# Projections cut into steps among local attention and level products in the second mixer of a two-block transformer kernel

## The chip, the cores and the metric

The kernel runs on one core of a Trainium2 chip, as one program. Time is device time in microseconds (us) of one execution. The profile is of one execution, taken by the hardware profiler; its times are microseconds from the start of the span unless a number is marked ns.

## What is computed

The input x has 512 positions of width 1024. A first block has a mixer (forgetting attention and chunked attention), attention over 256 memory rows and a feed-forward part. A second block has a mixer (below) and a layer that picks 16 x 8 of 16384 experts for each position. The change concerns the start of the program, where the memory rows are normed and projected, and the mixer of the second block:

```python
proj = h @ w_in[l]
aq, ak, av, gq, gk, gv, gg, glr = jnp.split(proj, split_points, axis=-1)
att = sliding_window_attention(aq, ak, av, attn_sinks[l])      # 8 heads, window 128
log_a = jax.nn.log_sigmoid(glr @ gla_gate_up[l] + gla_gate_bias[l]) / GLA_TAU
go = gla_chunked(gq, gk, gv, log_a)                            # 4 heads, linear attention with decay
go = rms_norm(go, gla_norm_w[l]).reshape(B, S, GLA_V_W) * jax.nn.silu(gg)
mixed = jnp.concatenate([att, go], axis=-1) @ w_out[l]
```

In `gla_chunked` position t takes from position s <= t the value of s by q_t . k_s times a decay, in each key channel the exponential of the difference of the summed log gates b at t and at s.

## The kernel before

Everything is in float32. A projection is three matmuls of float32r parts, high by high, low by high and high by low (`mm3`, lines 70 to 74), so each weight chunk that lands in `wraw` is first split: ScalarE copies the high part (`whi`, line 65), VectorE subtracts (`wlo`, line 66). `proj_T` gives transposed results: a chunk of 256 output columns is two groups of 8 x 3 matmuls with 512 moving columns, each into one PSUM bank, followed by a ScalarE copy (`evac`). `proj_rows` gives rows: for each of four 128-row tiles 8 x 3 matmuls. PSUM's eight banks are named by use: three `mm`, two `lg`, two `pt`, one `pv`. A bank is waited for when its turn comes again.

The code is written in program order; a scheduler that works when the kernel is built turns it into one fixed list of instructions for each engine, and an engine takes its list in order. What the lists are is shown below for three places.

**The second mixer** (`mixer2`). In the order of the code: two chunks of projections (key, gate input, `gq`), one for `gk`, the summed log gates `b`, two chunks of values (lines 751 to 754), the first query chunk (chunk 3), then for each half h: for h = 1 the second query chunk (chunk 4), and eight steps of `window` (local attention; two head pairs by four query tiles), each followed by one step of the generator `gla`, then two more steps of `gla`. Last come the two gate chunks 5 and 6 (`gg`), each followed by `silu_times`, and the split of the eight result tiles for the output projection (`row_hl`, lines 124 to 128).

A step of `window` (lines 659 to 699) does two logit matmuls, on VectorE a masked reduction, minimum, sum, reciprocal and scale, on ScalarE the exponentials, then transposes, a copy and the value matmuls. Eight steps of `gla` (lines 558 to 584) make the decay-weighted scores of 128 by 128 tiles: the diagonal first, and then seven levels. At level m = 1, 2, ... 64 a tile falls into blocks of 2m; pairs with t in the upper and s in the lower half of a block are this level's. The code takes the difference of b to the middle of the block for all positions (GpSimd, line 566), its absolute value and the exponential of minus that (ScalarE, 567 and 568), multiplies q by it (VectorE, 570) and k by it (GpSimd, 572), forms all 128 by 128 products for four tiles and two heads (TensorE, 578), and copies those of the level by a mask (VectorE, 583). The last two steps form the states that pass from tile to tile, the outputs and their norm (lines 587 to 634).

**The start.** `mem_kv` (line 388) sends the gain row g_mem_kv, then each memory tile, on SP's queue; the scheduler puts two weight chunks of w_mk ahead of the tiles. Each tile is squared (ScalarE, 93), normed (VectorE, 104), transposed (TensorE, 119), and split (ScalarE 121, VectorE 122) before w_mk is multiplied.

Of the kernel before, what the change touches and what calls it, by code (L numbers as in the profile page):

```python
# [8 lines left out]
F32 = mybir.dt.float32  # L9
# [9 lines left out]
S = 512  # L19
# [20 lines left out]
class Net:  # L40
# [89 lines left out]
    def proj_T(self, ws, x, nt, evacs, tags=("mm", "mm")):  # L130
# [127 lines left out]
    def mixer(self, hT):  # L258
        nc, a = self.nc, self.a
        with ExitStack() as c:  # L260
# [17 lines left out]
            def val(name, i):  # L278
# [5 lines left out]
                        [evac("fq", ch) for ch in range(2)], ("mm", "lg"))  # L284
# [103 lines left out]
    def mem_kv(self, mk_d, mv_d, between):  # L388

        nc, a = self.nc, self.a  # L390
        g = self.bcast_row(self.gain, a["g_mem_kv"], D, "gain", nc.sync)
        with ExitStack() as c:
            mp = c.enter_context(self.tc.tile_pool(reuse_waits="tile", name="memT", bufs=1))
            mT = Cols(mp, 2, tag="mT")
            for t in range(2):
                m = self.row.tile([128, D], F32, name="rowt")
                nc.sync.dma_start(m, a["mem"][0, t * 128:(t + 1) * 128, :])
                self.to_T(self.norm(m, g, None, m), mT, t)
# [5 lines left out]
            for ch in range(4):  # L404
                self.proj_T([self.weights(a["w_mk"][ch])], mT, 2, [evac(ch)])
# [8 lines left out]
    def mem_attention(self, hT, mk, mv):  # L414
        nc, a = self.nc, self.a
        with ExitStack() as c:
# [7 lines left out]
            self.proj_T([self.weights(a["w_mq"][ch]) for ch in range(2)], hT, NT, [evac(0), evac(1)], ("mm", "lg"))  # L424
# [30 lines left out]
    def feed_forward(self, hT, g, side, then):  # L455
        nc, a = self.nc, self.a
        with ExitStack() as c:
# [5 lines left out]
            for gr in range(8):  # L463
# [10 lines left out]
                if gr == 0:  # L474
                    self.proj_T(ws, hT, NT, [evac(0), evac(1)], ("mm", "lg"))
# [75 lines left out]
    def gla(self, qT, kT, b, v, gnw, outs, big, pp):  # L551
# [3 lines left out]
        for i in range(2):  # L555
            att = pp.tile([128, 2, NT, 128], F32, name="att", bufs=1)
            bi = b[:, i, :]
            for lev in range(-1, 7):
                if lev < 0:
                    ql, kl = qT[i], kT[i]  # L560
                else:
                    m = 1 << lev
                    e = pp.tile([128, S], F32, name="ge")
                    bv = bi.rearrange("p (n w) -> p n w", w=2 * m)
                    ev = e.rearrange("p (n w) -> p n w", w=2 * m)
# [3 lines left out]
                    ql = pp.tile([128, S], F32, name="gql")  # L569
                    nc.vector.tensor_mul(ql, qT[i], e)  # L570
                    kl = pp.tile([128, S], F32, name="gkl")
                    nc.gpsimd.tensor_mul(kl, kT[i], e)
                pss = [self.bank("mm").rearrange("p (a b) -> p a b", a=NT) for _ in range(2)]
# [5 lines left out]
                for j, ps in enumerate(pss):  # L579
                    if lev < 0:  # L580
                        nc.vector.tensor_mul(att[:, j], ps, self.ident[:, None, :].to_broadcast([128, NT, 128]))
                    else:
                        nc.vector.copy_predicated(
                            att[:, j], self.levmask[:, lev:lev + 1, :].to_broadcast([128, NT, 128]), ps)
                yield

            qb = pp.tile([128, S], F32, name="gql")
# [5 lines left out]
            kd = pp.tile([128, S], F32, name="gkl")  # L593
# [5 lines left out]
            kdT = pp.tile([128, NT - 1, 128], F32, name="ge")  # L599
# [16 lines left out]
            for j in range(2):  # L616
# [11 lines left out]
                sq = pp.tile([128, S], F32, name="gkl")  # L628
# [7 lines left out]
    def silu_times(self, o, g, pp):  # L636

        nc = self.nc
        e = pp.tile([128, S], F32, name="ge")
# [704 lines left out]
```

## Time and profile before

| | |
|---|---|
| median of three runs | 2433.2 us (2431.38 to 2435.75) |
| the profiled execution | 2440.6 us |
| its span | 2438.1 us |
| busy in the span: TensorE, VectorE, ScalarE, GpSimd | 97%, 72%, 41%, 23% |
| mean granted TensorE clock | 0.985 of full speed |

The profiled execution is 2.5 us longer than its span, for what lies around it. Busy time is a union of instruction times; matmuls overlap and their ends are modelled, so that the spacing of starts tells more than the length of one. The granted clock has two levels, 1.2 and 2.4 GHz; a share between 0.5 and 1 in a stretch is a mix of them.

### The profile page before, as it was taken

The page shows a single profiled execution, that of the slowest core. Times are in us where ns is not written, and L with a number is a line of the kernel's source. Part 1 is how long each engine was busy: PE and PEld are TensorE (multiplying, and loading weights), DVE is VectorE, ACT ScalarE, POOL GpSimd, SP SyncE. Part 2 cuts the span into 40 slices and gives each one's busy share as a digit, 9 for nine tenths or more (in the row PEclk, how much of TensorE's full clock was granted, in tenths as well). Part 3 has the DMA queues.
Part 4 walks back from the last instruction along what each step waited for, and adds up shares of the span by engine and source line. Part 5 has one row for each costly group of instructions (what it writes and reads, how often), then busy time and mean ns, then how long its engine had stood idle before and what let it go on. Part 6 is the DMA issues. An engine that isn't in the chain of part 4 may idle for free. (4 is left out here: it accounts for less than half of the span.)

```text
span 2438.1 us, 33761 instructions
## 1 busy us (share of the span) xinstructions
PE 2355.7 (97%) x12339; PEld 2005.8 (82%) x12339; DVE 1750.0 (72%) x3670; ACT 1010.1 (41%) x1656; POOL 550.8 (23%) x518
## 2 busy tenths in 40 slices
PE   6999999999999998998999899999999999999998
PEld 6866668788788887677988899888888888888887
DVE  5344554476565465766899999998988887988874
ACT  5344543443433334553333666433333343333332
POOL 2021010010010011212220000343434444444420
PEclk9999999999999999879999999999999999999999
DMA  6422223145454222013333455999888999999972
GB/s 259 139 87 70 70 104 108 48 182 201 178 193 152 97 76 87 18 35 143 101 113 125 184 215 213 335 322 328 298 308 325 348 342 346 340 351 335 334 286 77
DMA packets 163909, 479.83 MB, mean 197 GB/s; under 512 B 14968, under 2 KB 72328, under 8 KB 147488
## 3 DMA queue, kind: packets, MB, share of 16 engines
q1 hardware_dynamic: 119520, 317.76, 36.7%
q0 software_dynamic: 44224, 159.93, 18.2%
q8 instruction: 97, 1.59, 0.3%
q14 instruction: 68, 0.56, 0.1%
HBM read 438.85 MB, written 38.77 MB: 196 GB/s over the span
## 5 line engine op out<-in xcount | busy, mean ns | idle before, releaser
L65 ACT ACTIVATE whi<-wraw 128x1024 fp32r<-128x1024 f32 x430 | 446.9, 1048 | 650.5 <-PE hidT L73 288.2
L66 DVE TENSOR_TENSOR wlo<-wraw,whi 128x1024 fp32r<-128x1024 f32 x414 | 501.9, 1220 | 239.6 <-ACT whi L65 223.8
L72 PE MATMUL hidT<-hThi,whi 128*128 128x384 f32 x1024 | 346.5, 338 | 1.0 <-ACT aside L1030 1.0
L73 PE MATMUL hidT<-hTlo,whi 128*128 128x384 f32 x1024 | 345.1, 337 | 0.0
L74 PE MATMUL hidT<-hThi,wlo 128*128 128x384 f32 x1024 | 344.4, 336 | 0.0
L74 PE MATMUL o<-whi,al 128*128 128x512 f32 x768 | 300.6, 392 | 0.0
L73 PE MATMUL o<-wlo,ah 128*128 128x512 f32 x768 | 300.3, 391 | 0.0
L72 PE MATMUL o<-whi,ah 128*128 128x512 f32 x768 | 298.9, 389 | 1.1 <-ACT ah L1082 1.1
L967 POOL DMA_INDIRECT rows<-peer_u,ei x128 | 170.2, 1330 | 492.9 <-DVE ei L960 262.2
L967 POOL DMA_INDIRECT rows<-peer_v,ei x128 | 173.3, 1354 | 205.3 <-DVE ysparse L988 179.5
L73 PE MATMUL mm<-hTlo,whi 128*128 128x512 f32 (+1 forms) x560 | 207.8, 372 | 4.2 <-DVE hTlo L122 4.2
L72 PE MATMUL mm<-hThi,whi 128*128 128x512 f32 (+1 forms) x560 | 208.3, 374 | 1.7 <-ACT hThi L121 1.5
L74 PE MATMUL mm<-hThi,wlo 128*128 128x512 f32 (+1 forms) x560 | 208.1, 372 | 0.0
L72 PEld LDWEIGHTS hidT<-hThi,whi 128*128 128x128 f32 x1024 | 192.5, 188 | 4.8 <-ACT aside L1030 1.4
L73 PEld LDWEIGHTS hidT<-hTlo,whi 128*128 128x128 f32 x1024 | 192.4, 188 | 3.3
L74 PEld LDWEIGHTS hidT<-hThi,wlo 128*128 128x128 f32 x1024 | 192.3, 188 | 0.1
L74 PEld LDWEIGHTS o<-whi,al 128*128 128x128 f32 x768 | 144.0, 188 | 30.7 <-DVE al L1084 0.6
L72 PEld LDWEIGHTS o<-whi,ah 128*128 128x128 f32 x768 | 144.2, 188 | 29.8 <-ACT ah L1082 1.8
L73 PEld LDWEIGHTS o<-wlo,ah 128*128 128x128 f32 x768 | 144.1, 188 | 28.3
L988 DVE SCALAR_TENSOR_TENSOR ysparse<-rows,hid,ysparse 128x1024 f32<-128x1024 f32 x127 | 162.8, 1282 | 1.0
L976 DVE SCALAR_TENSOR_TENSOR rows<-rows,h2t 128x1024 f32<-128x1024 f32 x128 | 154.1, 1219 | 0.0
L1082 ACT ACTIVATE ah<-hs 128x384 fp32r<-128x384 f32 x96 | 50.3, 525 | 221.5 <-PE o L73 200.3
(401 smaller groups left out, 4504.2 us busy)
## 6 DMA issues: line engine op xcount, KB each, us to landing
wraw<-peer_uT SPq DMA_DIRECT2D x128, 512.0 KB
wraw<-peer_v SPq DMA_DIRECT2D x128, 512.0 KB
wraw<-w_ff SPq DMA_DIRECT2D x32, 1024.0 KB
wada<-w_ada SPq DMA_DIRECT2D x24, 1024.0 KB
gates_dense<-gst SPq DMA_DIRECT2D x24, 1024.0 KB
gj<-gates_dense SPq DMA_DIRECT2D x96, 256.0 KB
wraw<-w_in_qk SPq DMA_DIRECT2D x15, 1024.0 KB
wraw<-w_out SPq DMA_DIRECT2D x8, 1024.0 KB
```

Source lines behind the costliest of these rows:

```text
L65: nc.scalar.activation(hi[:, sl], raw[:, sl], AF.Copy)
L66: self.lo = (sub or nc.vector).tensor_sub(lo[:, sl], raw[:, sl], hi[:, sl].bitcast(F32))
L72: mm(ps, w[0], x[0], start=start, stop=False)
L73: mm(ps, w[0], x[1], start=False, stop=False)
L74: mm(ps, w[1], x[0], start=False, stop=stop)
L967: nc.gpsimd.indirect_dma_start(out=r, out_offset=None, in_=a["peer_v_2" if n else "peer_u_2"], in_offset=bass.IndirectOffsetOnAxis(ap=ei[k ...
L976: nc.vector.scalar_tensor_tensor(r, r, 1.0, h2, op0=OP.mult, op1=OP.mult, accum_out=hid[:, k:k + 1])
L988: nc.vector.scalar_tensor_tensor(y, r, hid[:, k:k + 1], y, op0=OP.mult, op1=OP.add)
L1082: nc.scalar.activation(ah, x, AF.Copy)
```

## The change

- `gla`: the levels work on halves of blocks. The difference to the middle is made for lower halves on GpSimd and for upper halves on VectorE, both with a sign that needs no absolute value; one exponential; k is multiplied in the lower halves and q in the upper halves, both on VectorE, into one tile `gw`. The products have the 64 upper positions of each tile as moving columns, and the masked copy writes those alone. Tiles `ge` and `gw` have three buffers.
- `mixer2`: the second value chunk, query chunk 4 and gate chunks 5 and 6 become a generator that gives after each three matmuls; between two steps of `window` and `gla` as many are taken as a share tells (by cost 4.6 in the first half, 4 in the second, where a step costs 0.65 or 1). `silu_times` is called as soon as its inputs are there.
- PSUM: the three `mm` banks become two `mm` and one `mx`. Where no name is given, they are taken in turn (mm, mm, mx); `gla` names `mm`, the new steps name `mx`.
- `mem_kv`: both memory tiles are sent first on SP's queue, and the gain row and the first weights are to be issued after them. Tiles for constants have a pool of their own.

```diff
-    BANKS = {"mm": 3, "lg": 2, "pt": 2, "pv": 1}
+    BANKS = {"mm": 2, "mx": 1, "lg": 2, "pt": 2, "pv": 1}
-    def bank(self, tag="mm"):
+    def bank(self, tag=None):
+        if tag is None:
+            tag = ("mm", "mm", "mx")[self.turn % 3]
+            self.turn += 1
...
     def mem_kv(self, mk_d, mv_d, between):
-        g = self.bcast_row(self.gain, a["g_mem_kv"], D, "gain", nc.sync)
+            ms = [self.row.tile([128, D], F32, name="rowt") for _ in range(2)]
+            for t, m in enumerate(ms):
+                read = nc.sync.dma_start(m, a["mem"][0, t * 128:(t + 1) * 128, :])
+            with self.tc.issue_after(read.ins):
+                g = self.bcast_row(self.gain, a["g_mem_kv"], D, "gain", nc.sync)
...
+            with self.tc.issue_after(read.ins):
+                first = self.weights(a["w_mk"][0])
...
     def gla(self, qT, kT, b, v, gnw, outs, big, pp):
-                    nc.gpsimd.tensor_sub(ev, bv, bv[:, :, m - 1:m].to_broadcast([128, S // (2 * m), 2 * m]))
-                    nc.scalar.activation(e, e, AF.Abs)
-                    nc.scalar.activation(e, e, AF.Exp, scale=-1.0)
-                    nc.vector.tensor_mul(ql, qT[i], e)
-                    nc.gpsimd.tensor_mul(kl, kT[i], e)
+                nc.gpsimd.tensor_sub(e0, mid, b0)
+                nc.vector.tensor_sub(e1, b1, mid)
+                nc.scalar.activation(e, e, AF.Exp)
+                nc.vector.tensor_mul(w0, halves(kT[i])[0], e0)
+                nc.vector.tensor_mul(w1, halves(qT[i])[1], e1)
+                pss = [self.bank("mm")[:, 0:256].rearrange("p (a b) -> p a b", a=NT) for _ in range(2)]
...
-                        nc.tensor.matmul(pss[j][:, t, :], kl[r, c], ql[r, c], start=True, stop=True)
+                        nc.tensor.matmul(pss[j][:, t, :].rearrange("p (n w) -> p n w", w=m), w[r, c],
+                                         halves(w[r, c])[1], start=True, stop=True)
...
     def mixer2(self, hT):
-            for i in range(2):
-                ws = [self.weights(a["w_in_v_2"][i, 0]), self.weights(a["w_in_v_2"][i, 1])]
-                self.proj_rows(ws, hT, NT, lambda t, ps: nc.scalar.activation(
-                    v[:, t, i * 320:(i + 1) * 320], ps, AF.Copy))
+            self.proj_rows(v_chunks(0), hT, NT, v_evac(0))
...
+            def slices():
+                ws = v_chunks(1)
+                ahead = self.weights(a["w_in_qk_2"][4])
+                for t in range(NT):
+                    ps = self.bank("mx")[:, :320]
+                    for k in range(8):
+                        w = ws[k // 4]
+                        self.mm3(ps, hT.tile(t, k), (w[0][:, k % 4, :], w[1][:, k % 4, :]), k == 0, k == 7)
+                        yield 0.65
+                    v_evac(1)(t, ps)
+                for ch, evac in ((4, keep(("aq2", "aq3"), -0.125)), (5, keep(("gg0", "gg1"), -1.0)),
+                                 (6, keep(("gg2", "gg3"), -1.0))):
...
+                            yield 1.0
+                        evac(m, ps)
...
+            share = (4 * 8 * 0.65 + 16) / 8, 32 / 8
             for h in range(2):
-                if h:
-                    proj(4, ("aq2", "aq3"), -0.125)
+                owed = 0.0
                 for _ in self.window((2 * h, 2 * h + 1), T("aq", 2 * h + 2), kT, v, sink, nsink, pp):
                     next(gla)
+                    owed += share[h]
+                    while owed > 0.5:
+                        owed -= next(rest, 99.0)
+                    gate()
...
-            for h in range(2):
-                names = (f"gg{2 * h}", f"gg{2 * h + 1}")
-                proj(5 + h, names, -1.0)
-                for i in range(2):
-                    self.silu_times(go[2 * h + i], tiles[names[i]], pp)
```

Line numbers move: `mm3` is at 73 to 77 after the change, the weight split at 68 and 69, the local attention at 674 to 714. TensorE's list where local attention begins, before (`lg` logits, `pt` transposes, `pv` values; `mm` level products):

```order
L670 MATMUL lg<-akT,aq_7602 128x128 x2
L578 MATMUL mm<-gq_7214,gk_7276 128x128 x8
L670 MATMUL lg<-akT,aq_7602 128x256 x2
L578 MATMUL mm<-gql,gkl 128x128 x4
L689 MATMUL pt<-ident,wp 128x128
L578 MATMUL mm<-gql,gkl 128x128 x3
```

and some rows further on in the same place of the changed kernel:

```order
L704 MATMUL pt<-ident,wp 128x128
L685 MATMUL lg<-akT,aq_7486 128x256 x2
L709 MATMUL pv<-wpT,v_7327 64x128 x2
L593 MATMUL mm<-gw 128x64 x8
L75 MATMUL mx<-whi,hThi 128x320
L76 MATMUL mx<-wlo,hThi 128x320
L77 MATMUL mx<-whi,hTlo 128x320
L685 MATMUL lg<-akT,aq_7486 128x256 x2
```

The level products have 64 columns, and the three matmuls of a value step (`mx`) stand between attention and level matmuls.

SP's queue at the start, before:

```order
L87 DMA gain<-g_mem_kv 128x1024
L60 DMA wraw<-w_mk 128x2048 x2
L397 DMA rowt<-mem 128x1024 x2
L60 DMA wraw<-w_mk 128x2048 x2
L1233 DMA xin<-x 128x1024 x4
```

and of the changed kernel:

```order
L397 DMA rowt<-mem 128x1024 x2
L90 DMA gain<-g_mem_kv 128x1024
L63 DMA wraw<-w_mk 128x2048 x2
L1293 DMA xin<-x 128x1024 x2
L63 DMA wraw<-w_mk 128x2048
L1293 DMA xin<-x 128x1024
```

The memory tiles went from behind two weight chunks to the front, and tiles of x stand between the later chunks.

ScalarE's list at the start, before (`junk` are the squares, `mThi` the high parts of the normed memory):

```order
L65 ACTIVATE whi<-wraw 128x1024 x4
L93 ACTIVATE junk,ms<-rowt 128x512 x4
L121 ACTIVATE mThi<-pt 128x512
L65 ACTIVATE whi<-wraw 128x1024
L121 ACTIVATE mThi<-pt 128x512
```

and of the changed kernel:

```order
L96 ACTIVATE junk,ms<-rowt 128x512 x4
L68 ACTIVATE whi<-wraw 128x1024 x2
L124 ACTIVATE mThi<-pt 128x512 x2
L68 ACTIVATE whi<-wraw 128x1024 x2
L96 ACTIVATE junk,ms<-xin 128x512
L124 ACTIVATE mThi<-pt 128x512 x2
```

The squares stand ahead of all weight copies, and the second chunk's copies stand ahead of the second tile's.

## Rows read from the trace of the kernel before

**Rows 1.** The page: busy time by engine (part 1), granted clock in 40 slices (part 2).

```profile
PE 2355.7 (97%) x12339; PEld 2005.8 (82%) x12339; DVE 1750.0 (72%) x3670; ACT 1010.1 (41%) x1656; POOL 550.8 (23%) x518
...
PEclk9999999999999999879999999999999999999999
```

**Rows 2.** Stretches, core 0: from:to, us, busy by engine (instructions), clock, DMA.

```profile
932.80:951.08 18.28, 14.22 (x84) 14.00 (x85) 4.39 (x5) 8.56 (x14) 2.60 (x3) 0.91 0.30 115
951.08:962.08 11.00, 11.00 (x51) 8.83 (x49) 4.16 (x4) 3.39 (x6) 0.00 (x0) 1.00 0.49 194
962.08:999.60 37.52, 31.14 (x236) 21.07 (x235) 33.17 (x118) 22.29 (x67) 10.36 (x9) 0.86 0.08 29
999.60:1020.94 21.34, 21.34 (x101) 15.48 (x100) 10.24 (x18) 12.80 (x23) 7.80 (x7) 1.00 0.00 0
1020.94:1064.32 43.38, 40.35 (x236) 27.38 (x235) 35.20 (x118) 22.74 (x67) 10.37 (x9) 0.61 0.08 25
1064.32:1096.20 31.88, 31.88 (x147) 24.44 (x147) 14.76 (x25) 19.15 (x33) 4.92 (x4) 1.00 0.09 33
```

**Rows 3.** Timeline, TensorE, projections: start, us, line, op, [idle <- releaser].

```profile
937.27 0.41 PE L73 MATMUL mm<-wlo,hThi 128*128 128x320 f32 x1 [0.85 <-DVE wlo L66]
...
954.73 0.39 PE L73 MATMUL mm<-hTlo,whi 128*128 128x512 f32 x1
...
961.76 0.39 PE L74 MATMUL mm<-hThi,wlo 128*128 128x512 f32 x1
```

**Rows 4.** Timeline, TensorE, local attention and the levels.

```profile
962.40 1.06 PE L578 MATMUL mm<-gq,gk 64*128 64x128 f32 x16
963.29 0.60 PE L670 MATMUL lg<-akT,aq 64*128 64x256 f32 x4
963.73 0.38 PE L578 MATMUL mm<-gql,gkl 64*128 64x128 f32 x2
...
974.72 0.44 PE L689 MATMUL pt<-ident,wp 128*128 128x128 f32 x2
975.09 0.94 PE L578 MATMUL mm<-gql,gkl 64*128 64x128 f32 x12
...
1003.26 0.66 PE L694 MATMUL pv<-wpT,v 128*64 128x128 f32 x8
1003.85 1.13 PE L606 MATMUL pt<-v,ge 128*128 128x256 f32 x4
```

**Rows 5.** Stretches of 5 us, 985 to 995.

```profile
985.00:990.00 5.00, 3.81 (x22) 1.97 (x18) 4.95 (x22) 2.55 (x9) 1.27 (x1) 0.91 0.49 197
990.00:995.00 5.00, 5.00 (x29) 3.38 (x30) 3.02 (x16) 2.25 (x10) 0.00 (x0) 0.50 0.00 0
```

**Rows 6.** Groups by line, VectorE, 962 to 1101: count | busy us, mean ns | idle.

```profile
L583 DVE COPY_PREDICATED att<-levmask,mm 128x512 f32<-128x512 uint32 x28 | 20.1, 727 | 5.2 <-PE mm L578 5.2
...
L570 DVE TENSOR_TENSOR gql<-gq,ge 128x512 f32<-128x512 f32 x12 | 9.5, 795 | 6.2 <-PE pv L623 5.7 <-ACT ge L568 0.5
...
L677 DVE CUSTOM_DVE_ANT_0 wp<-lg,wmask 128x256 f32<-128x256 f32 x24 | 10.0, 416 | 5.7 <-PE pt L689 5.5
...
L677 DVE CUSTOM_DVE_ANT_0 wp<-lg,wmask 128x128 f32<-128x128 f32 x8 | 2.1, 283 | 8.5 <-PE lg L670 8.5
```

**Rows 7.** Groups by line, ScalarE, 962 to 1101.

```profile
L722 ACT ACTIVATE gg<-mm 128x512 f32<-128x512 f32 x4 | 2.3, 586 | 1.2 <-PE mm L74 1.2
```

**Rows 8.** Timeline, all engines, the start.

```profile
12.37 2.00 ACT L65 ACTIVATE whi<-wraw 128x1024 fp32r<-128x1024 f32 x2 [2.45 <-DMA wraw<-w_mk]
...
14.28 0.61 ACT L93 ACTIVATE junk<-rowt 128x512 bf16<-128x512 f32 x1
...
23.43 0.99 PE L72 MATMUL mm<-mThi,whi 128*128 128x256 f32 x3
...
23.81 0.60 ACT L121 ACTIVATE mThi<-pt 128x512 fp32r<-128x512 f32 x1 [1.15 <-PE pt L119]
```

**Rows 9.** Timeline, TensorE, the join with the output projection.

```profile
1103.18 0.50 PE L72 MATMUL mm<-whi,hThi 128*128 128x512 f32 x1 [0.20 <-ACT hThi L127]
```

More of the change, by code (lines that the diff above doesn't have):

```diff
@@ L404, in mem_kv @@
             for ch in range(4):
-                self.proj_T([self.weights(a["w_mk"][ch])], mT, 2, [evac(ch)])
+                self.proj_T([self.weights(a["w_mk"][ch]) if ch else first], mT, 2, [evac(ch)])
             nc.gpsimd.dma_start(mk_d, mk)
@@ L577, in gla @@
                         r = slice(64 * j, 64 * j + 64)
-                        nc.tensor.matmul(pss[j][:, t, :], kl[r, c], ql[r, c], start=True, stop=True)
[L579 to L584, printed above, removed]
+                        nc.tensor.matmul(pss[j][:, t, :].rearrange("p (n w) -> p n w", w=m), w[r, c],
+                                         halves(w[r, c])[1], start=True, stop=True)
+                mask = halves(self.levmask[:, lev, :])[1][:, None].to_broadcast([128, NT, 64 // m, m])
+                for j in range(2):
+                    nc.vector.copy_predicated(
+                        att[:, j].rearrange("p t (n h w) -> p t n h w", h=2, w=m)[:, :, :, 1, :], mask,
+                        pss[j].rearrange("p t (n w) -> p t n w", w=m))
                 yield
-            qb = pp.tile([128, S], F32, name="gql")
+            qb = pp.tile([128, S], F32, name="gw", bufs=3)
             nc.scalar.activation(qb, bi, AF.Exp)
@@ L762, in mixer2 @@
             proj(3, ("aq0", "aq1"), -0.125)
+            def slices():
+                ws = v_chunks(1)
+                ahead = self.weights(a["w_in_qk_2"][4])
+                for t in range(NT):
+                    ps = self.bank("mx")[:, :320]
[6 more added lines that the diff above has]
+                                 (6, keep(("gg2", "gg3"), -1.0))):
+                    w = ahead
+                    if ch < 6:
+                        ahead = self.weights(a["w_in_qk_2"][ch + 1])
+                    for m in range(2):
+                        ps = self.bank("mx")
+                        sl = slice(m * 128, (m + 1) * 128)
+                        for k in range(8):
+                            self.mm3(ps.rearrange("p (t n) -> p t n", n=128), (w[0][:, k, sl], w[1][:, k, sl]),
+                                     hT.span(0, NT, k), k == 0, k == 7)
+                            yield 1.0
+                        evac(m, ps)
@@ L763, in mixer2, with gate @@
+            rest = slices()
+            gated = 0
+            def gate():
+                nonlocal gated
+                while gated < len(go) and f"gg{gated}" in tiles:
+                    self.silu_times(go[gated], tiles[f"gg{gated}"], pp)
+                    gated += 1
+            share = (4 * 8 * 0.65 + 16) / 8, 32 / 8
             for h in range(2):
-                if h:
-                    proj(4, ("aq2", "aq3"), -0.125)
+                owed = 0.0
                 for _ in self.window((2 * h, 2 * h + 1), T("aq", 2 * h + 2), kT, v, sink, nsink, pp):
@@ L767, in mixer2 @@
                     next(gla)
+                    owed += share[h]
+                    while owed > 0.5:
+                        owed -= next(rest, 99.0)
+                    gate()
+                if h:
+                    for _ in rest:
+                        pass
+                else:
+                    while "aq3" not in tiles:
+                        next(rest)
                 for _ in range(2):
                     next(gla)
-            for h in range(2):
-                names = (f"gg{2 * h}", f"gg{2 * h + 1}")
-                proj(5 + h, names, -1.0)
-                for i in range(2):
-                    self.silu_times(go[2 * h + i], tiles[names[i]], pp)
+                    gate()
@@ L1194, in before_peer @@
         make_identity(nc, self.ident)
-        ones = self.row.tile([128, 128], F32, name="rowt")
+        setup = ctx.enter_context(ExitStack())
+        sp = setup.enter_context(tc.tile_pool(reuse_waits="tile", name="setup", bufs=1))
+        ones = sp.tile([128, 128], F32, name="ones_f")
         nc.gpsimd.memset(ones, 1.0)
@@ L1212, in before_peer @@
         nc.vector.tensor_copy(self.iotaf, ii)
+        setup.close()
         def gain(name):
```

55 lines of the change are left out of this document (31 added, 24 removed).

## The prediction

> **What bounds the kernel now.** I read the page first: TensorE is busy 97% of the span, and the row of granted clocks shows two of its 40 slices below full speed [rows 1]. An average that high says that nearly all work hides under TensorE, so a gain must be a place where TensorE waits, runs at its lower level, or does needless work. The low slices are the 17th and 18th, 975 to 1097 us at 61 us a slice, in the second mixer, so the next view was a table of stretches there [rows 2]. The reader is to see a stage cut in two kinds of time: stretches of projections alone, where the clock stays at 1.00 and TensorE is always busy, and two stretches of local attention with the level products (37.52 and 43.38 us), where VectorE is busy 33.17 and 35.20 us, TensorE has idle time, and the mean granted clock is 0.86 and 0.61. So in those two stretches VectorE and its answers set the pace, and in the others TensorE does; neither helps the other. The 5 us table shows how the clock goes: in a piece with TensorE 3.81 us busy of 5 it begins to fall, and in the next it reads 0.50, which is 1.2 GHz of 2.4 [rows 5]. Last I read the timeline of the start [rows 8]: the first projection stands at 23.43 us, when the last mThi copy is under way.
>
> What the reference point is: the profiled execution took 2440.6 us, 7.4 above the median of 2433.2. I take differences from the profile and subtract them from the median. About 0.2% (5 us) is what a measurement of this kernel can tell from no change.
>
> **The second mixer.** The end of the first value projection (932.8) to the first matmul of the output projection (1096.2) is 18.28 + 11.00 + 37.52 + 21.34 + 43.38 + 31.88 = 163.4 us [rows 2]. In the new order the query projection of chunk 3 still stands alone (11.0), and all else is one mixed stretch. I add up TensorE's work in it at the full clock.
>
> - Moved projections. Chunks 4, 5 and 6 are 48 matmuls of 512 columns each; 31 spacings between 954.73 and 961.76 are 0.227 us each [rows 3], so 144 x 0.227 = 32.7. The second value chunk ran from 936.0 to 951.08, part of it at the lower level; 13.8 us from 937.27 on for 95 of 96 matmuls is 0.145 each, so 14.0 at most [rows 3].
> - The ends of the two level loops (transposes, states, outputs, norms). The stretch 999.60 to 1020.94 holds 48 projection matmuls, so 21.34 - 10.9 = 10.4; the stretch to 1096.2 holds 96, so 31.88 - 21.8 = 10.1 [rows 2].
> - One local-attention stretch at the full clock. From above: the busy time corrected for the clock. A mean of 0.86 is 28% of the time at half speed, so 31.14 - 5.2 = 25.9; 0.61 is 78%, so 40.35 - 16.9 = 23.4 [rows 2]; small waits inside are in these. From below, by spacings: 16 records of the first product in 0.89 us, 4 of the logits in 0.44, 2 transposes in 0.37, 8 of the values in 0.59 [rows 4]. Per half that is 0.9 for the first product, 32 of the logits at 0.11 = 3.5, 28 transposes at 0.185 = 5.2, 56 value records at 0.074 = 4.1, and 112 level records at 0.056 = 6.3, together 20.0.
> - The level products keep their number and lose half their columns. The trace has them with 128 columns only, so the price of a half lies between 3.1 and 6.3. I take 6.3, the row of the same product with the same weights as it stands, so 20 us for a half, with 16.9 and 24.6 (the mean of 25.9 and 23.4) as ends. The Trainium skill ("TensorE: Matmul & The Clock Gate", section "LDWEIGHTS (loading the stationary operand)") says that a weight load costs by its own columns, 128 here as before, whatever is multiplied; that speaks against the halved columns. By it they buy nothing and the sum is the one below; by columns alone it would be 6.3 us shorter, and the time 2384. No run so far shows which.
>
> Sum of TensorE: 32.7 + 14.0 + 10.4 + 10.1 + 2 x 20 = 107.2 us.
>
> VectorE in the same region: 33.17 + 10.24 + 35.20 + 14.76 = 93.4 us busy [rows 2]. A level now costs 0.795 + 2 x 0.727 = 2.25 us there; the two products move to half tiles, one difference comes over from GpSimd, and the masked copies halve. A 128-element step of the logits' reduction costs 0.416 - 0.283 = 0.133, so some 0.15 us of each instruction does not shrink [rows 6]; half tiles are then about 0.47 and 0.44, and a level 3 x 0.47 + 2 x 0.44 = 2.3. VectorE gets no relief from the halves: 14 x 0.05 = under 1 us more. What shrinks is ScalarE (one exponential of 512 for two passes) and GpSimd (half a difference, no product), and neither is on the path there. So VectorE needs 94 us and TensorE 107: the mixed stretch becomes TensorE's, with VectorE 12% below it. The order shows that the steps really stand between the attention instructions, mostly three to eleven projection matmuls at a time.
>
> What the mixing adds. The steps have one bank (mx), so after each of 10 groups the next group waits for ScalarE's copy, 0.586 us [rows 7], when nothing else stands between: 5.9. From above it is that copy and one weight conversion of 1.0 us (two took 2.00 [rows 8]) ahead of it in ScalarE's order, 15.9; from below 0, since the order often puts attention matmuls there. I take 5.9. At the end, the last norm and gate are nine 128x512 instructions at 0.59 to 0.80, 5.3 to 7 us [rows 6, 7]; behind the last norm's matmul the order has some 40 output matmuls (9 us) that don't need them. Before, that join cost 0.20 [rows 9]. I take 2, from 0 to 7. The 4.1 us of waiting at 932.8 [rows 2] goes: weights of the second value chunk stood behind level exponentials on ScalarE, and now the projection of chunk 3 comes there, whose weights are converted earlier.
>
> New region: 11.0 + 107.2 + 5.9 + 2 = 126.1, so 163.4 - 126.1 = **37.3 us less**. Ends: 11 + 67.2 + 2 x 16.9 = 112 (51 less) and 11 + 67.2 + 2 x 24.6 + 15.9 + 7 = 150.3 (13 less).
>
> **The start.** Now ScalarE converts both first chunks of w_mk (the second is there at 12.37), and only then squares the memory tiles (14.28); the first projection stands at 23.43, the last mThi copy at 23.81 [rows 8]. In the new order the two memory tiles, 1 MB, lead the queue, the squares come first on ScalarE, and their norm and transposes lie in the time in which the weights arrive. What is late next is the second chunk of w_mk, still behind the same 3.6 MB: ready at about 12.4 to 13, converted by 15, with the second tile's mThi copies behind it, so the first projection at 16 to 17.5. That gives 6 to 7.4. The x tiles' loads come between the chunks now, which could hold the third chunk back, and GpSimd's gain row shares the same bytes. I take **6**; ends 3 (the second chunk 3 us later) and 8. The four x tiles are pushed behind by one chunk each, hidden by the projections of w_mk (192 matmuls, over 20 us).
>
> **At nothing.** The bank rotation (mm, mm, mx) is three banks in turn, as before; outside the second mixer no order depends on it. The setup tiles free two row buffers; nothing on the path waits for them. SP's queue has one more chunk between the halves of the value weights; the six stretches moved 0 to 194 GB/s [rows 2], so there is room.
>
> **Sum.** 37.3 + 6 = 43.3; 2440.6 - 43.3 = 2397.3 by the profiled execution, **2390 us** by the median.
>
> **The rivals.**
> 1. The forecast: a TensorE-bound mixed stretch at the full clock, 2390, ends 2380 to 2400. For it: always a projection to issue while VectorE answers, and the clock stood at 1.00 wherever projections did. Chance 0.58.
> 2. The clock still falls for a while. Now some 10 us of the first and 34 of the second stretch ran at half speed, 22 us lost. If the mixed stretch has it as long, 2390 + 22 = 2412. For it: the clock fell while TensorE was still 3.81 us of 5 busy [rows 5], so it needs no long idle stretch. Against it: projections now fill most of the time, and it read 1.00 wherever they did [rows 2]. Chance 0.14.
> 3. In-order waits: steps placed by a planner's guess meet late answers from VectorE and ScalarE, the upper ends of the sum, 150.3 and a start of 3: 2433.2 - 13 - 3 = 2417. Chance 0.12.
> 4. Better: the level products halve fully, the bank's hand-over is always covered: 2433.2 - 51 - 8 = 2374. Chance 0.09.
> 5. Slower: the granted clock is 1.2 GHz for most of the mixed stretch. All of it would add 107 us, 2497. It decides from 43 us of full-speed work done at half speed, some 86 us of the stretch. Single steps of three matmuls among half-array products look like the two stretches that lost it. Chance 0.04.
> 6. It doesn't do what it says: VectorE keeps the pace, the steps only fill its waits and then stretch it, and the start is bound by the same bytes. Within 5 us of 2433. Chance 0.03.
>
> **How the numbers follow.** Faster 0.93 (cases 1 to 4), same 0.03, slower 0.04. The range takes in cases 1 and 4 down to 2372, and case 2 with most of case 3 up to 2413; beyond lie case 5, 6 and the tail of 3.
>
> **What would show it.** Right: the first projection at 16 to 18 us; 932.8-to-output stretch of 120 to 135 us; PEclk at 9 in all slices of the second mixer; VectorE busy about 94 of those; ScalarE's exponentials of a level once. Wrong: PEclk under 0.9 there (case 2, 5), TensorE waits on att, wp or mx evacuations of over 20 us in sum (case 3), or the start still beyond 21 us. A change of the time behind the output projection would be a surprise, as nothing there is touched.

## The result, and the profile after

The changed kernel takes **2404.4 us** (median of four runs, 2401.66 to 2405.01) against 2434.5 for the kernel before beside it (2431.38 to 2438.12): ratio 0.9877, 95% interval 0.9864 to 0.9889, 30.1 us less. The forecast was 2390, and its range held the result, though not the ends (2380 to 2400) of the case that it took as likeliest. The profiled execution took 2401.7 us (span 2399.6), 2.7 below its median; that of before, 2440.6, lay 6.1 above its own.

The page of the changed kernel (answers to [rows 1]):

```profile
PE 2333.1 (97%) x12339; PEld 1987.6 (83%) x12339; DVE 1742.0 (73%) x3698; ACT 1000.1 (42%) x1642; POOL 519.4 (22%) x504
...
PEclk9999999999999999999999999999999999999999
```

The timeline of its start (answers to [rows 8]):

```profile
4.63 0.63 ACT L96 ACTIVATE junk<-rowt 128x512 bf16<-128x512 f32 x1 [2.62 <-DMA rowt<-mem]
...
12.97 1.99 ACT L68 ACTIVATE whi<-wraw 128x1024 fp32r<-128x1024 f32 x2
...
14.54 1.97 PE L122 MATMUL pt<-ident,rowt 128*128 128x128 f32 x8 [2.10 <-DVE mTlo L125]
...
15.95 1.20 ACT L124 ACTIVATE mThi<-pt 128x512 fp32r<-128x512 f32 x2
...
16.58 0.79 PE L75 MATMUL mm<-mThi,whi 128*128 128x256 f32 x2
```

Its second mixer in stretches (columns as in [rows 2]): the first value chunk, chunk 3, the mixed stretch up to the end of the last norm's matmul, and the rest up to the first expert matmul:

```profile
908.21:922.40 14.19, 14.19 (x98) 14.19 (x98) 12.45 (x19) 7.20 (x12) 3.67 (x5) 1.00 0.14 47
922.40:933.39 10.99, 10.99 (x50) 8.82 (x49) 5.42 (x9) 5.11 (x10) 1.26 (x2) 1.00 0.51 185
933.39:1060.67 127.28, 124.89 (x833) 91.93 (x832) 88.16 (x298) 76.44 (x188) 11.35 (x12) 1.00 0.12 43
1060.67:1126.20 65.53, 58.05 (x310) 48.96 (x308) 39.15 (x54) 21.22 (x38) 18.61 (x21) 0.95 0.38 133
```

TensorE's waits from 933 to 1075, all of them:

```profile
PE pt L704 <- DVE wp L702: 1.2, 2, 0.6
PE mm L75 <- ACT hThi L130: 1.0, 2, 0.5
PE mx L75 <- ACT aq L737: 0.6, 2, 0.4
PE lg L685 <- DVE mx L692: 0.4, 1, 0.4
PE mm L75 <- DVE rowt L1211: 0.2, 1, 0.2
```

Where the time went, by the two profiles: the first value chunk starts at 908.21 instead of 916.67, 8.5 us earlier. Of these the start gave 6.6, still 6.6 at 140 us. The rest appeared between 320 and 426 us, where nothing was changed; kernels of the study that keep the old start show some 2 to 3 us there too, so it belongs to the profiled run of before. From the first value chunk to the first expert matmul it took 218.0 us instead of 247.9, 29.9 less; behind that the offset stays at 38.5. In the mixed stretch the clock no longer falls, TensorE is busy nearly throughout, and its waits are 2.2 us. (Behind it, in the last of the four stretches, the clock falls for a while in both kernels: 0.95.) Still the mixed stretch is longer than forecast: 122.1 us without the 21 output matmuls that stand in it, where 113.1 were forecast.

### The profile page after: what moved, and what is told of

The parts are those of the page before. It is cut to its first block, busy times and chain, and to the rows that moved or that the text cites. A ratio compares the mean times of both kernels' runs of the same rounds, so it can differ in the third digit from the quotient of the medians.

```text
span 2399.6 us, 33734 instructions
## 1 busy us (share of the span) xinstructions
PE 2333.1 (97%) x12339; PEld 1987.6 (83%) x12339; DVE 1742.0 (73%) x3698; ACT 1000.1 (42%) x1642; POOL 519.4 (22%) x504
## 5 line engine op out<-in xcount | busy, mean ns | idle before, releaser
L1023 POOL DMA_INDIRECT rows<-peer_v,ei x128 | 165.8, 1295 | 212.8 <-DVE ysparse L1044 187.7
L76 PE MATMUL mm<-hTlo,whi 128*128 128x512 f32 (+1 forms) x368 | 134.4, 365 | 4.6 <-DVE hTlo L125 4.6
L75 PE MATMUL mm<-hThi,whi 128*128 128x512 f32 (+1 forms) x368 | 134.6, 367 | 1.7 <-ACT hThi L124 1.4
L77 PE MATMUL mm<-hThi,wlo 128*128 128x512 f32 (+1 forms) x368 | 134.5, 366 | 0.0
```

What stands on the lines that cost most here:

```text
L75: mm(ps, w[0], x[0], start=start, stop=False)
L76: mm(ps, w[0], x[1], start=False, stop=False)
L77: mm(ps, w[1], x[0], start=False, stop=stop)
L1023: nc.gpsimd.indirect_dma_start(out=r, out_offset=None, in_=a["peer_v_2" if n else "peer_u_2"], in_offset=bass.IndirectOffsetOnAxis(ap=ei[k ...
```

## The experiments

Each kernel ran beside the kernel before, and ratios are to that, with a 95% interval in brackets. "Over the changed kernel" is a difference of two medians; where the two ratios say something else, their difference stands beside it.

### The parts alone

**The start alone**: the diff's parts in `mem_kv` and the setup.

> The kernel before with the start of the change alone (memory tiles first in SP's queue, the two small setup tiles in their own pool). My theory: the first mk evacuation came 7.1 us earlier in the changed kernel's profile and the offset stayed at 6.6 up to the first mixer, so the whole kernel becomes 6 to 7 us shorter: 2428 against 2434.5. Rival: the weights' bytes set the start, the gain is given back where the x tiles now arrive later, and the 6.6 belongs to the second mixer's profile or to the run: within 2 us of the kernel before.

2425.6 us, ratio 0.9967 (0.9951 to 0.9983), 8 us less by the ratio. **The second mixer alone**: all the rest of the diff.

> The changed kernel with the start of before, so the second mixer's change alone. My theory: the two parts touch nothing in common and add up, so this gives the whole gain of 30.1 less the start's 6 to 7: 23 to 24 us less than before, 2410 to 2411. Rival: the profiles' difference in the second mixer, 29.9 us, is right and the start gives nothing in the median: 2404.

2410.6 us, ratio 0.9904 (0.9888 to 0.9920), 23.4 us less. The two add up to 31.4 against 30.1 for both, so no interplay of the parts can be seen within the intervals (some 4 us each way), and the 29.9 of the profiles is more than the 23.4 that the second mixer gives in the median, since the profiled run of before lay above its median.

**Half-tile levels alone**: `gla` and `silu_times` of the change in the kernel before.

> The kernel before with half-tile levels alone: no steps, three mm banks, the old order and the old start. My theory: VectorE's work of a level stays as it is (three products of some 0.47 and two masked copies of 0.44 against 0.795 and two of 0.727), and the level products keep their price, so the local-attention stretches keep their pace: between 2429 and 2436. Rival A: what counts there is the way from one level to the next, and one pass of ScalarE instead of two and a shorter masked copy take 0.5 to 1 us from each of 14 levels, so 2420 to 2427. Rival B: TensorE gets still less work a microsecond, its clock falls for longer, and it is slower by 3 to 10 us, 2437 to 2444.

2447.5 us, ratio 1.0052 (1.0035 to 1.0068): **12.7 us slower**, rival B. Its two local-attention stretches:

```profile
956.75:999.35 42.60, 40.12 (x236) 27.85 (x235) 26.39 (x121) 19.04 (x61) 0.61 (x1) 0.57 0.03 5
1022.83:1067.62 44.79, 42.66 (x235) 29.69 (x234) 27.70 (x124) 20.71 (x64) 0.61 (x1) 0.56 0.03 6
```

Against [rows 2], VectorE is busy 26.4 instead of 33.2 us and GpSimd 0.6 instead of 10.4, so the halves did relieve VectorE, which the prediction denied. But the clock is 0.57 instead of 0.86, and the first stretch is 42.6 instead of 37.5 us. TensorE, at 1.2 GHz for most of it, is now what the others wait for: VectorE's masked copies sit behind the level products for 16.2 us instead of the 5.2 of [rows 6]. Groups of VectorE from 956.75 to 1067.6:

```profile
L590 DVE COPY_PREDICATED att<-levmask,mm 128x256 f32<-128x256 uint32 x26 | 13.1, 519 | 16.2 <-PE mm L586 16.2
...
L693 DVE TENSOR_TENSOR sum<-sum,es 128x1 f32<-128x1 f32 x32 | 4.9, 152 | 1.7 <-ACT es L692 1.7
```

Part of VectorE's relief can be read in the kernel before, at one place of its timeline:

```profile
967.96 1.27 POOL L572 TENSOR_TENSOR gkl<-gk,ge 128x512 f32<-128x512 f32 x1 [32.56 <-ACT wpT L691]
...
968.00 1.23 DVE L685 TENSOR_TENSOR sum<-sum,es 128x1 f32<-128x1 f32 x1
```

The group of that sum in the kernel before, from 962.08 to 1064.3:

```profile
L685 DVE TENSOR_TENSOR sum<-sum,es 128x1 f32<-128x1 f32 x32 | 12.0, 376 | 0.5 <-ACT es L684 0.4
```

A sum of 128x1 elements (median of 32: 156 ns) takes 1.23 us and ends with GpSimd's product. All 32 took 12.0 us before and 4.9 with halves alone, where GpSimd has no product: 7.1 of the 14.3 us that VectorE's busy time fell by in the two stretches. The Trainium skill ("SBUF — State Buffer", section "SBUF: two separate sides") says that VectorE and GpSimd share a pair of ports as an exclusive lock, held for a whole instruction, also when VectorE's instruction has two inputs in SBUF and GpSimd's reads SBUF; this row agrees.

**Steps with full-tile levels**: `gla` and `silu_times` of before in the changed kernel.

> The changed kernel with the full-tile levels of before: steps, banks and start as changed. My theory: TensorE sets the pace of the mixed stretch, and VectorE's work is the same either way, so the halves give little there: 2402 to 2408 against the changed kernel's 2404.4. Rival: the longer preparation of a level (two passes of ScalarE, a product on GpSimd, a masked copy of 0.73) makes TensorE wait or VectorE the bound: 2412 to 2425.

2420.2 us, ratio 0.9940 (0.9926 to 0.9954), 15.8 over the changed kernel: the rival was right. The clock is 1.00 throughout the mixed stretch, but TensorE's largest waits and some of VectorE's groups there are these:

```profile
PE pt L696 <- DVE wp L694: 7.5, 11, 1.8
PE mm L585 <- DVE att L590: 1.5, 1, 1.5
```

```profile
L590 DVE COPY_PREDICATED att<-levmask,mm 128x512 f32<-128x512 uint32 x28 | 19.6, 735 | 7.3 <-PE mm L585 7.3
...
L577 DVE TENSOR_TENSOR gql<-gq,ge 128x512 f32<-128x512 f32 x12 | 11.7, 978 | 0.0
...
L692 DVE TENSOR_TENSOR sum<-sum,es 128x1 f32<-128x1 f32 x32 | 8.5, 267 | 4.4 <-ACT es L691 4.3
```

Waits sum to 11.1 us instead of 2.2, and the stretch up to the last norm is 141.0 instead of 127.3. So the halves, with the third buffer of `ge` and `gw` that is part of them, are worth 16 us with steps and cost 13 without; steps with full tiles are worth 5 to 7 (2420.2 against the start alone at 2425.6, or by the ratios 14.6 less 8.0). Neither part alone does what both do.

### Two changes to the levels

**Level products at 128 columns** in the changed kernel:

```diff
-matmul(pss[j][:, t, :].rearrange(...), w[r, c], halves(w[r, c])[1], start=True, stop=True)
+matmul(pss[j][:, t, :], w[r, c], w[r, c], start=True, stop=True)
```

> The changed kernel with the level products at 128 moving columns again (same weights, same masked copies of half tiles; the other half of each product is not used). My theory: a level product costs the same at 64 and at 128 columns. In the changed kernel's trace runs of 16, 8 and 4 of them between other work took 1.04, 0.59 and 0.37 us, 0.055 each; before, 16 records of the first product took 0.89. So 224 of them give 0 to 1 us: 2402 to 2407. The Trainium skill ("TensorE: Matmul & The Clock Gate", section "LDWEIGHTS (loading the stationary operand)") says that a weight load costs by its own columns, 128 in both kernels, which is this result. Rival: the price goes by moving columns, 0.028 for 64 more at 0.227 us for 512, and 224 x 0.028 = 6.3 us more: 2411.

2411.0 us, ratio 0.9899 (0.9882 to 0.9915), 6.6 over the changed kernel; by the ratios 5.4, and their intervals overlap. That is the rival's number, but its mechanism shows in small part only. A run of 16 products with 128 columns, and one with 64 in the changed kernel:

```profile
972.76 1.16 PE L593 MATMUL mm<-gw 64*128 64x128 f32 x16
973.86 0.50 PE L75 MATMUL mx<-hThi,whi 128*128 128x512 f32 x1
```

```profile
1032.00 1.11 PE L593 MATMUL mm<-gw 64*128 64x64 f32 x16
1033.04 0.50 PE L75 MATMUL mx<-hThi,whi 128*128 128x512 f32 x1
```

Up to the next matmul they take 1.10 and 1.04 us; the shortest runs of 8 take 0.64 and 0.59. Eight products more cost about 0.45 us in both, so one costs 0.056 at either width, where the rival has 0.028 more; only a run as a whole is 0.05 longer. The Trainium skill ("TensorE: Matmul & The Clock Gate", section "LDWEIGHTS (loading the stationary operand)") says that a weight load costs by its own columns, 128 in both kernels; the equal price agrees. Of the 7.5 us by which the mixed stretch grew, 3.5 are waits: the built order came out differently, and TensorE waits 5.1 us for VectorE's softmax instead of 1.2. Another 3.3 stand at the level products (by spacings 20.7 us for all instead of 17.3): 1.5 are the 0.05 of 30 runs, and the rest are runs that took longer, four runs of 8 0.82 us and one 1.20. Why they did stays open. So the halved columns are worth 1.5 us as far as this run shows, not the 6.3 of the rival.

**One of a level's products on GpSimd** (`nc.gpsimd.tensor_mul(w1, ...)`).

> The changed kernel with the second product of each level on GpSimd instead of VectorE. Theory A: what made full-tile levels 16 us dearer in the steps was GpSimd working beside VectorE (the 128x1 sum took 376 ns in the kernel before, 152 with halves alone, where GpSimd was busy 0.6 us instead of 10.4 in the same stretch), so VectorE loses what it gives away and GpSimd is slower at it: 2407 to 2415. Theory B: it was only the amount of VectorE's work or the length of a level; VectorE gives up 14 products of 0.474, 6.6 us, and the time stays or falls: 2398 to 2405.

2411.0 us, ratio 0.9895 (0.9876 to 0.9915), 6.6 over the changed kernel; by the ratios 4.4, and their intervals overlap. It is theory A's number by another way. VectorE did get rid of the work: from 933 to 1070 it is busy 87.4 us instead of 93.7, 6.3 less where theory B has 6.6. TensorE waits only 1.1 us in the mixed stretch, but the clock fell once (5 us pieces):

```profile
1030.00:1035.00 5.00, 4.66 (x24) 3.02 (x25) 4.49 (x16) 3.57 (x11) 2.97 (x4) 0.82 0.00 0
1035.00:1040.00 5.00, 5.00 (x28) 3.35 (x27) 3.80 (x9) 1.50 (x5) 2.42 (x2) 0.50 0.16 36
1040.00:1045.00 5.00, 5.00 (x11) 2.52 (x12) 2.01 (x10) 0.60 (x1) 0.00 (x0) 0.50 0.41 174
1045.00:1050.00 5.00, 5.00 (x38) 3.83 (x37) 3.10 (x12) 3.51 (x10) 0.00 (x0) 0.81 0.02 3
```

(0.18 + 0.50 + 0.50 + 0.19) x 5 = 6.9 us of full-speed work lost, as much as the whole difference. So A's mechanism is not seen here, and B's gain is not either; what of GpSimd's part made full tiles dearer stays open. The run shows that rival 2 of the prediction was near.

### The missing 8 us: changes of the array's shape

The changed kernel's TensorE around one group of value matmuls (their part of the array is 128 by 64, that of the projections 128 by 128), and a later place with transposes among projections:

```profile
945.47 0.31 PE L75 MATMUL mx<-whi,hThi 128*128 128x320 f32 x1
945.62 0.31 PE L76 MATMUL mx<-wlo,hThi 128*128 128x320 f32 x1
945.76 0.31 PE L77 MATMUL mx<-whi,hTlo 128*128 128x320 f32 x1
946.00 0.66 PE L709 MATMUL pv<-wpT,v 128*64 128x128 f32 x8
946.59 0.41 PE L75 MATMUL mx<-whi,hThi 128*128 128x320 f32 x1
946.84 0.31 PE L76 MATMUL mx<-wlo,hThi 128*128 128x320 f32 x1
946.99 0.31 PE L77 MATMUL mx<-whi,hTlo 128*128 128x320 f32 x1
947.14 0.38 PE L704 MATMUL pt<-ident,wp 128*128 128x128 f32 x2
...
978.17 0.38 PE L704 MATMUL pt<-ident,wp 128*128 128x128 f32 x2
978.31 0.48 PE L75 MATMUL mx<-hThi,whi 128*128 128x512 f32 x1
978.63 0.38 PE L704 MATMUL pt<-ident,wp 128*128 128x128 f32 x2
```

Projections follow each other by 0.147 us. The last before the group has 0.24, the group 0.59 where 8 x 0.055 is 0.44, the first behind it 0.25: three times about 0.1 to 0.15, and no wait is listed. Before a transpose, which is 128*128 too, the spacing stays at 0.15. Behind two transposes the next projection takes 0.32 instead of 0.23, but the two take only 0.14, where two in a run of transposes take 0.22 (0.109 each): together that is no dearer. So what costs is the change of shape and not the change of work. Why a change of shape costs this, no row shows. From the first logits to the last norm the order has 126 changes between neighbours of 128*128, 64*128 and 128*64.

**Few changes**: `window` is pipelined over its steps, with one softmax buffer more, the preparation of a level stands a step ahead of its products, and the driver pins the order on TensorE (the loop, shortened):

```diff
+with issue_after(last_projection):
+    next(win)     # values of two steps ago, this step's logits
+    next(gla)     # 16 level products
+next(win)         # softmax on VectorE and ScalarE
+steps(2.0)        # half of the projections, issued after those products
+next(win)         # transposes of the step before
+steps(2.0)
```

> The changed kernel with local attention pipelined over its steps and the order pinned on TensorE: in each of 16 steps the values of two steps ago, the logits of this one and the level's 16 products stand together, then all projection matmuls of the step with the transposes of the step before in their middle. The same matmuls; changes of the array's shape (128*128, 64*128, 128*64) between neighbours fall from 126 to 84, and one softmax buffer more is used. My theory: what I sized too small is a price for each change of shape. A projection before a 64-row product is spaced 0.33 instead of 0.227, a run of 16 level products takes 0.15 more than 16 x 0.0555, and the projection behind it up to 0.1 more: 0.1 to 0.17 for a change, so 42 fewer give 4 to 7 us: 2397 to 2400. Rival A: the price is waits on VectorE and banks that the trace puts elsewhere; then pinning takes the freedom to fill them, and it is 2405 to 2415. Rival B: VectorE, some 5.5 us a step, is the bound already: within 3 us of 2404.4.

2407.7 us, ratio 0.9885 (0.9867 to 0.9904): no better than the changed kernel, as rival A or B would have it, but the trace says why. The second mixer is 4.8 us shorter, and the expert layer, which nobody touched, 10.8 us longer. To find room for a larger buffer I had dropped an unused 8-element tile from the constants. **That tile alone**, taken from the changed kernel:

> The changed kernel without the 8-element tile in its constants, nothing else. My theory: an address effect of 32 bytes alone, 10.8 us behind the second mixer, so 2413 to 2416. Rival: the tile does nothing and the 10.8 us belonged to the pinned order: 2403 to 2406.

2414.0 us, ratio 0.9904 (0.9889 to 0.9920), 9.6 over the changed kernel; by the ratios 6.6, and their intervals just touch. The trace is clearer. First and last expert matmul of the first kind in this kernel, with the minimum, median and maximum length of 1024:

```profile
L75 PE MATMUL hidT<-hThi,whi x1024: 333/336/445, 1127.0 to 2387.9; 128*128 128x384 f32 x171
```

and in the changed kernel:

```profile
L75 PE MATMUL hidT<-hThi,whi x1024: 331/334/442, 1126.2 to 2376.1; 128*128 128x384 f32 x171
```

1260.9 against 1249.9 us, 0.9% more. The eleven kernels here that have the tile took 1248.5 to 1251.3 us for this, whatever else was changed in them, and the three without it 1260.8 to 1261.1, so it is the tile. **The pinned version with that tile back** (two small tiles of the mixer became one to make room):

> The pipelined, pinned version again, with the 8-element tile back in the constants that it had given up for the larger softmax buffer (the bytes come from two small tiles of the mixer instead). In its trace the second mixer, from the copy of the attention keys to the first expert matmul, took 233.9 us against the changed kernel's 238.7, but from there to the last expert matmul of the first kind 1260.7 against 1249.9. My theory: the missing 32 bytes moved every later tile, the matmuls of the last stage ran 2 to 3% wider apart, and with the bytes back the 10.8 us go: 2396 to 2401. Rival: it was the pinned order, by way of what arrives later, or the chip: 2405 to 2410 again.

**2396.4 us** (2395.90 to 2398.75), ratio 0.9834 (0.9819 to 0.9849): 8.0 less than the changed kernel, 10.5 by the ratios, whose intervals don't touch. No kernel of the study is faster beyond its spread. Its mixed stretch is 119.5 us up to the last norm, where the changed kernel has 127.3 (columns as in [rows 2]):

```profile
935.44:1054.91 119.47, 114.87 (x826) 89.37 (x826) 86.84 (x297) 77.01 (x188) 11.38 (x12) 1.00 0.13 46
```

Local attention with the levels takes 41.0 us of it by the spacings, the changed kernel's 47.0. Since the pipelining came with the order, these 8 us are not the price of 42 changes alone; the next kernel sets the number of changes apart.

**More changes**: the order of the few-changes kernel (without the tile), with projections between values, logits and each half of a level's products.

> As the pipelined, pinned version, but with projections put between the values, the logits and the two halves of a level's products: the same matmuls, changes of shape 147 instead of 84. My theory: 63 more changes at 0.1 to 0.17 us, 6 to 11 us above the pinned version with few changes: 2403 to 2411 if that one is at 2397 to 2400. Rival: a change costs nothing and only waits count; then finer mixing covers them better and this is no slower than the other.

2421.2 us, ratio 0.9946 (0.9928 to 0.9963), 13.4 over the few-changes kernel without the tile. The mixed stretch of that one, and then of this:

```profile
936.25:1057.87 121.62, 117.65 (x827) 91.35 (x827) 86.03 (x297) 77.15 (x188) 11.19 (x12) 0.97 0.12 44
```

```profile
932.55:1067.25 134.70, 129.86 (x830) 88.85 (x830) 89.01 (x298) 76.73 (x188) 10.93 (x12) 0.96 0.12 41
```

The stretch grew by 13.1 us. Of these 0.9 are waits, 1.7 are lost to the clock, which dipped in both (3.4 and 5.1 us lost), and 0.7 are three output matmuls more that stand in it. The other 9.8 over 63 changes is **0.16 us each**.

**Two products swapped at the loop ends**, on top of the best version:

> As the pinned version with the 32 bytes back, and at the end of each level loop the two products of the third tile in the other order, so that neighbours of one shape stand together: 76 changes of shape instead of 84. My theory: 8 x 0.1 to 0.2 us, so 1 to 2 us less than that version, and 5 to 8 less than the changed kernel: 2395 to 2400. Rival: those chains wait on VectorE's states, and the order of two matmuls gives nothing: the same as the other.

2396.3 us (2391.31 to 2405.22), ratio 0.9834 (0.9813 to 0.9855). The stretch is 117.9 instead of 119.5 us, as 8 changes less at 0.2 would have it; in the median nothing can be told.

### What made the halves slower

**Halves alone plus useless work**:

```diff
 next(gla)
+junk = self.bank("mm")
+for n in range(8):
+    matmul(junk, hT.tile(0, n)[0], hT.span(0, NT, n)[0], start=n == 0, stop=n == 7)
```

> The kernel before with half-tile levels alone, which was 12.7 us slower than before, plus useless work: 8 matmuls of 512 columns on TensorE after each of the 16 steps of local attention, 128 x 0.227 = 29 us, into a bank that nobody reads. My theory: halves alone took 7 us off VectorE in each stretch, and it got longer all the same because the clock there was 0.57 and 0.56; with the junk the clock stays near 1.00, TensorE's sum for a stretch is 20 + 14.5 and some 3 for changes of shape, 37 to 39 instead of 42.6 and 44.8, and the loop ends behind lose less too: 2430 to 2438, so 10 to 17 less than halves alone in spite of 29 us more work. Rival: the stretch is bound by the way from level to level, whatever the clock; then the junk fills waits at best and the time is 2445 to 2475.

2437.1 us, ratio 1.0006 (0.9994 to 1.0017): 10.5 us **less** than halves alone, with 29 us more work. Its two stretches:

```profile
956.63:999.48 42.85, 42.13 (x305) 30.54 (x304) 30.20 (x127) 19.78 (x63) 3.40 (x4) 0.96 0.07 25
...
1020.21:1061.51 41.30, 40.57 (x304) 29.45 (x304) 29.70 (x125) 19.77 (x63) 1.94 (x2) 1.00 0.07 27
```

The clock is 0.96 and 1.00 instead of 0.57 and 0.56. The stretches came out above the 37 to 39 that I had expected, so the gain inside them is 3.2 us; some 2.8 came in the first loop end (20.7 instead of 23.5) and 2.9 between the second loop and the output's transposes (70.1 instead of 72.9), where with halves alone the projections begin at half speed. With the clock held, 14.5 us more work fit into a stretch of about the same time, so the clock is shown as what made halves alone slow. What in the halves let it fall is not shown: the products have half the columns, and the pace changed too, and no run separates the two. As an estimate, 41.3 less 64 x 0.227 leaves 26.8 us for one half of local attention at full clock when it is mixed.

## Why the prediction was right, and where it was not

**The range.** It held 2404.4, but by its width: the case of the forecast ended at 2400, and the range reached further for a falling clock (case 2) and for waits (case 3), neither of which came. What went wrong is in the forecast's own sum.

**Start.** The time was right: forecast 6, by the start of the first projections in the profiles 6.6, alone 8.0 with an interval of some 4 either way; the first projection stands at 16.58 (forecast 16 to 17.5), and at 16.5 to 18.5 in the other kernels with the new start. The path was only in part the one forecast. ScalarE did convert the second chunk by 15 (12.97 + 1.99), but the second tile's transposes stood until 14.54 waiting for VectorE (mTlo), whose list had the first chunk's split ahead of it, and the tile's copy at 15.95 came behind those transposes and a square of x.

**TensorE's sum in the mixed stretch** is the step that was mis-sized. By spacings (each matmul is charged the time to the next one's start, listed waits taken out), from 933.39 to the last norm:

| | forecast | measured |
|---|---|---|
| chunks 4 to 6, 144 matmuls | 32.7 | 38.9 (0.270 each) |
| second value chunk | 14.0 | 16.8 |
| loop ends | 20.5 | 17.2 |
| local attention and levels, both halves | 40.0 | 47.0 |
| TensorE's sum | 107.2 | 119.9 |
| waits: bank; VectorE | 5.9; none | 0.6; 1.6 |

With 21 output matmuls (5.2 us) that already stand in it, 119.9 + 2.2 + 5.2 is the 127.3 of the stretch. The prediction took most of its spacings from inside runs of one kind and added them up as if the order of the kinds were free. What the 126 changes cost was in its own rows: in [rows 4], 8 value matmuls take 0.59 us between others. The prediction used that for the values (8.2 forecast, 8.5 measured), but the first product, the logits and the level products went in at the price inside a run: 1.8, 7.0 and 12.6 us, where 3.7, 10.8 and 17.3 were measured. The transposes went in too high (10.4, measured 6.5), since they now stand among projections of their own shape. The other estimate that it had, busy time corrected for the clock (24.6), was nearer to the 23.5 of a half; 20 is what the pinned version, with long runs, comes down to (20.5).

The 14.0 for the second value chunk rests on a misreading: of its 96 matmuls 84 stand between 936.0 and 951.08, part of them at the lower clock, and 12 ran before 932.8. That 96 at 0.147 are 14.1 all the same is luck.

**The bank's hand-over** (5.9, measured 0.6) and **the join** (2, measured 1.2) were priced too high. Less the 1.6 of waits for VectorE, which had no term, that gave back a third of the 12.7: 123.3 us in all against 115.1, so the region gave 29.1 us instead of 37.3. With 1.9 from the 12 matmuls that no longer stand in the first value chunk, and 1.2 lost between the region and the experts, these are roughly the 29.9 of the profiles.

**The halves.** "VectorE gets no relief" was wrong: with halves alone VectorE's busy time fell from 33.2 and 35.2 to 26.4 and 27.7 us. A level's own instructions cost about what was forecast: in the changed kernel the masked copies and the differences more than the 0.44 and 0.47, the products a little less (0.43 and 0.42):

```profile
L597 DVE COPY_PREDICATED att<-levmask,mm 128x256 f32<-128x256 uint32 x28 | 13.5, 525 | 7.9 <-PE mm L593 7.8
...
L584 DVE TENSOR_TENSOR ge<-b 128x256 f32<-128x256 f32 x8 | 5.0, 629 | 0.0
```

What the prediction had no term for is that GpSimd's products no longer hold up VectorE's small instructions. VectorE's sum still came out as forecast (94; measured 93.7 from 933 to 1070), though the 128x1 sums in it fell from 12.0 to 5.7 us: that is in part luck. That TensorE gains next to nothing by halved columns held, within the 1.5 us above.

**The reference.** Differences were taken from a profiled run of before that lay 6.1 us above its median, in part by more time at the low clock, and subtracted from the median. Of the 13.2 us between the saving forecast (43.3) and the one measured (30.1), 8.8 are this and the changed kernel's profiled run, which lay 2.7 below its own median; the profiles differ by 38.9 where 43.3 was forecast.

**Rivals.** The clock stays at 1.00 in the mixed stretch, so 2 and 5 did not come; halves alone and the product on GpSimd show their mechanism at work a small edit away. Rival 3's in-order waits came only with full tiles (11 us). Rival 4's 2374 was out of reach, as halved columns give, as far as shown, 1.5 of the 6.3 us that it has for them. Rival 6 did not come either: VectorE is busy 88.2 of the 127.3 us. Behind the output projection nothing moved.

## What to carry to other kernels

When work is interleaved on TensorE, count how often neighbours change the array's shape and price each change from the trace (0.1 to 0.2 us here); group half-array products into one run a step and let full-array transposes ride with the projections. Where an engine other than TensorE sets the pace and TensorE idles, an edit that relieves that engine and thins out TensorE's work may let the clock fall and make the kernel slower, as here by 12.7 us: give TensorE real work in the same edit. After an edit that moves memory, look at stages that were not touched before judging the edit.

## What was not expected of the hardware

- 32 bytes fewer in front of all later tiles in a partition made the matmuls of the expert layer some 2 ns longer, and 1260.9 us out of its 1249.9. Why stays open.
- A 128x1 sum on VectorE took 1.23 us instead of 0.16 while GpSimd did a 128x512 product.
- 128 useless matmuls, 29 us of work, made a kernel 10.5 us faster by holding the clock.
- A change of the array's shape between neighbouring matmuls took 0.16 us on average, with no wait listed.
